# Residual add and RMS norm on one core: x and results moved in two interleaved partition groups in place of four, and the last residual on SyncE's queue

## The chip, the cores and the metric

One core of a Trainium2 chip. The metric is device time in microseconds (us), the median of several runs.

## The reference

x and residual are [32, 2048, 2048] float32, 537 MB each, and so is the output.

```python
z = x + residual
rms = np.sqrt(np.mean(z ** 2, axis=-1, keepdims=True) + eps)
return (z / rms * gamma).astype(np.float32)
```

## The kernel before

The 65,536 rows go through in 65 tiles. Tiles 1 to 63 have 128 partitions x 8 rows (8 MB each of x, residual and output); tile 0 has 3 rows a partition and tile 64 has 5. There are two buffers `z` for x, which also become the output in place, and one area for the residual. Three engines' programs carry it. SyncE moves x and the output:

```python
Q = 4
def group(q):
    return slice(q, P, Q)          # every fourth partition

def sp_turn(sp, i):
    def load(q):
        sp.wait_ge(s_out[q], i * U)      # store group q of tile i-1 has landed
        load_x(sp, i + 1, q)             # into the same partitions of the same buffer
    Turn(i).wait(sp, "done", -1)         # tile i-1 is computed
    for q in range(Q):
        store(sp, i - 1, q)
    for q in range(Q):
        load(q)
```

`sp_turn` is unrolled for i from 1 to 63. VectorE waits for x and residual of a tile, adds in three parts (`add_a`, `add_b`, `add_c`) and later scales. ScalarE squares and sums, and issues the residual of the next tile as soon as the adds have freed its place:

```python
def act_turn(s, t, chain):
    ...
    t.wait(s, "add_a")
    squares(s, chain, z[p], a, m, ssq[p][0], 0)
    if i == last - 1:
        load_r(s, t, 1)              # the last residual, on ScalarE's queue
    elif i:
        t.wait(s, "add_b")
        load_r(s, t, 1)
    ...
```

At the end SyncE stores tile 63 in two halves by rows, and tile 64 in three parts.

## Time and profile before

| | before |
|---|---|
| time | 3732.35 us (3732.1 to 3732.79, 4 runs) |
| bytes moved | 1610.73 MB, mean 432 GB/s |
| VectorE busy | 2300.7 us, 62% |
| ScalarE busy | 1059.7 us, 28% |
| data DMAs | 517 on SyncE's queue, 63 on ScalarE's |
| a tile's period | 58.00 to 58.02 us early, 58.16 us late |

Read it from the DMA rows: compute has room, DMA has none (its two data queues take 67.3% and 32.6% of the engines' time). The page's lines stand in the prediction. One that is not there is that of the queue which the profile names "instruction"; its columns are packets, MB and share of 16 engines' time:

```profile
q14 instruction: 7, 0.05, 0.0%
```

It looks like nothing. It matters below, because its packets take time from data: the one at 1426 us lasts 0.31 us, and the 64 KB packet that follows it on its engine 2.83 us in place of 2.42. (Six of the seven are of 8 KB and come during the run; one of 40 bytes comes at the start.) What the packets hold the trace does not show; that their number goes with the length of SyncE's program was my reading of their distance of 930 us.

### The profile page before, as it was taken

How to read it: one execution, taken by the hardware profiler on the slowest of the kernel's cores; microseconds unless marked ns; L12 is line 12 of the kernel's file. 1: busy time of each engine (PE TensorE's matmuls, PEld its weight loads, DVE VectorE, ACT ScalarE, POOL GpSimd, SP SyncE). 2: the span in 40 equal slices, each digit the busy share in tenths (PEclk: the TensorE clock that was granted, in tenths of full speed). 3: DMA queues.
4: the chain of work that ended last, by engine and by line, in shares of the span. 5: the costliest groups of instructions: out<-in, count | busy, mean ns of one | idle time of the engine just before them, and what ended most of it. 6: DMA issues, size and time to landing. Idle time of an engine off the chain costs nothing.

```text
span 3730.9 us, 4005 instructions
## 1 busy us (share of the span) xinstructions
DVE 2300.7 (62%) x842; ACT 1059.7 (28%) x1157; POOL 0.2 (0%) x4
## 2 busy tenths in 40 slices
DVE  5657566575665756657556575565755657556566
ACT  2323233232331322313223132231322313223132
POOL 0000000000000000000000000000000000000000
DMA  9999999999999999999999999999999999999998
GB/s 421 433 436 429 436 432 433 437 430 437 430 436 436 431 436 430 436 433 433 437 430 436 433 433 437 430 436 431 434 436 430 438 430 436 434 432 429 435 429 377
DMA packets 34695, 1610.73 MB, mean 432 GB/s; under 512 B 9281, under 2 KB 9345, under 8 KB 9345
## 3 DMA queue, kind: packets, MB, share of 16 engines
q1 hardware_dynamic: 25616, 1085.34, 67.3%
q10 hardware_dynamic: 9072, 525.34, 32.6%
q14 instruction: 7, 0.05, 0.0%
HBM read 1073.77 MB, written 536.87 MB: 432 GB/s over the span
## 4 chain that ended last, share of the span: by engine, by line
DMA 65%; DVE 27%; issue 5%; SPq 1%; ACT 1%; another core or an unknown queue 1%; ACTq 0%; DVEq 0%
DMA out_dram<-z 33%; DMA z<-in_x_dram 30%; DVE z L193 13%; DVE z L198 13%; SPq L170 1%; DMA r_area<-in_residual_dram 1%; ACT sq_junk L244 0%; DMA z<-in_gamma_dram 0%; ACTq L161 0%; DVE rstd L217 0%; ACT rms L254 0%; DVEq L314 0%; DVEq L139 0%; SPq L290 0%
## 5 line engine op out<-in xcount | busy, mean ns | idle before, releaser
L193 DVE TENSOR_TENSOR z<-z,r_area 128x8192 f32<-128x8192 f32 (+2 forms) x192 | 1104.8, 5810 | 1339.8 <-DMA z<-in_x_dram 1325.1
L244 ACT ACTIVATE sq_junk<-z 128x2048 f32<-128x2048 f32 x512 | 962.1, 1879 | 2640.9 <-DVE z L193 2630.7
L198 DVE SCALAR_TENSOR_TENSOR z<-z,rstd,gamma_tile 128x2048 f32<-128x2048 f32 x507 | 1156.5, 2344 | 4.5
L244 ACT ACTIVATION_READ_ACCUMULATOR sq_junk<-z 128x1 f32 x512 | 95.4, 186 | 0.0
L217 DVE RECIPROCAL rstd<-rms 128x4 f32<-128x4 f32 (+1 forms) x128 | 22.4, 175 | 58.2 <-ACT rms L254 58.2
L254 ACT ACTIVATE rms<-ssq,eps_tile 128x4 f32<-128x4 f32 (+1 forms) x128 | 38.0, 297 | 11.7
L198 DVE SCALAR_TENSOR_TENSOR z<-z,tail_rstd,gamma_tile 128x2048 f32<-128x2048 f32 x5 | 11.6, 2346 | 0.1
L311 DVE LOAD_MASK_SELECT gamma_tile<-z x1 | 0.0, 14 | 16.2 <-DMA z<-in_gamma_dram 16.2
L193 DVE TENSOR_TENSOR z<-z 128x2048 f32<-128x2048 f32 x3 | 6.7, 2284 | 0.0
L311 DVE STREAM_SHUFFLE gamma_tile<-z 128x2048 f32<-128x2048 f32 x1 | 2.3, 2290 | 0.0
L309 DVE MEMSET z<- 128x2048 f32 x1 | 1.8, 1765 | 0.4 <-issue 0.4
L244 ACT ACT_TABLE_LOAD x1 | 1.3, 1283 | 0.9 <-SPq L80 0.9
L254 ACT ACT_TABLE_LOAD x1 | 1.3, 1283 | 0.1
L254 ACT ACTIVATE tail_rms<-tail_ssq,eps_tile 128x2 f32<-128x2 f32 (+1 forms) x3 | 0.9, 295 | 0.1
L308 DVE MEMSET eps_tile<- 128x1 f32 x1 | 0.1, 59 | 1.0 <-SPq L80 1.0
L327 DVE RECIPROCAL tail_rstd<-tail_rms 128x2 f32<-128x2 f32 (+1 forms) x3 | 0.5, 158 | 0.0
L381 POOL MEMSET const-bfloat16-1.0<- 128x1 bf16 x1 | 0.1, 101 | 0.0
L381 POOL MEMSET const-uint8-127<- 128x1 uint8 x1 | 0.1, 101 | 0.0
L381 POOL MEMSET const-float32-0.0<- 128x1 f32 x1 | 0.1, 98 | 0.2 <-issue 0.2
L381 POOL MEMSET const-float32-1.0<- 128x1 f32 x1 | 0.1, 98 | 0.0
## 6 DMA issues: line engine op xcount, KB each, us to landing
out_dram<-z SPq DMA_DIRECT2D x2, 4096.0 KB, 27.5
z<-in_x_dram SPq DMA_DIRECT2D x4, 1280.0 KB
r_area<-in_residual_dram ACTq DMA_DIRECT2D x1, 5120.0 KB, 25.6
out_dram<-z SPq DMA_DIRECT2D x2, 2048.0 KB, 8.7
z<-in_x_dram SPq DMA_DIRECT2D x249
out_dram<-z SPq DMA_DIRECT2D x248, 30.6
z<-in_x_dram SPq DMA_DIRECT2D x1, 3072.0 KB
z<-in_residual_dram SPq DMA_DIRECT2D x1, 3072.0 KB, 17.2
```

Of the source, the lines that this page charges most:

```text
L170: sp.dma_start(out=rows(o_f, i)[group(q)], in_=z[i % 2][group(q), : sizes[i], :]).then_inc(s_out[q], U)
L193: return v.tensor_add(out=s, in0=s, in1=res(i, a, b))
L198: ins = v.scalar_tensor_tensor(out=s, in0=s, scalar=rs[:, c + g - a : c + g - a + 1], in1=gamma_tile[:, :], op0=mult, op1=mult,)
L217: v.reciprocal(out=rstd[p][h][:, :n], in_=rms[p][h][:, :n]).then_inc(dve, U)
L244: s.activation(out=sq_junk[:, :], in_=src[:, g, :], func=Act.Square, accum_out=sq[:, c + g - a : c + g - a + 1],)
L254: return s.activation(out=rm, in_=sq, func=Act.Sqrt, bias=eps_tile[:, :], scale=inv_d)
L308: v.memset(eps_tile[:, :], float(eps))
L309: v.memset(stage, 0.0).then_inc(tail_ev["add"], 1)
L311: v.stream_shuffle(gamma_tile[:, :].rearrange("p (a b) -> p a b", a=16), stage, [0] * 32)
L327: v.reciprocal(out=tail_rstd[:, a:b], in_=tail_rms[:, a:b]).then_inc(dve, U)
L381: nc = _bacc.Bacc("TRN2", target_bir_lowering=False, num_devices=1)
```

## The change

The intent is to move the same bytes with fewer DMAs. Two things change: the group count, and who issues the last tile's residual.

```diff
-    Q = 4
+    Q = 2
...
         for q in range(Q):
             store(sp, i - 1, q)
         for q in range(Q):
+            if i == last - 1 and q == Q // 2:
+                Turn(i).wait(sp, "add_a")
+                load_r(sp, Turn(i), 1)
             load(q)
...
-        if i == last - 1:
-            load_r(s, t, 1)
-        elif i:
+        if 0 < i < last - 1:
             t.wait(s, "add_b")
             load_r(s, t, 1)
```

## The prediction

> **What bounds the kernel now.** I read the page first: busy shares, the strip of 40 slices, the DMA queues.
>
> ```profile
> span 3730.9 us, 4005 instructions
> DVE 2300.7 (62%) x842; ACT 1059.7 (28%) x1157; POOL 0.2 (0%) x4
> DMA  9999999999999999999999999999999999999998
> GB/s 421 433 436 429 436 432 433 437 430 437 430 436 436 431 436 430 436 433 433 437 430 436 433 433 437 430 436 431 434 436 430 438 430 436 434 432 429 435 429 377
> DMA packets 34695, 1610.73 MB, mean 432 GB/s; under 512 B 9281, under 2 KB 9345, under 8 KB 9345
> q1 hardware_dynamic: 25616, 1085.34, 67.3%
> q10 hardware_dynamic: 9072, 525.34, 32.6%
> ```
>
> No compute engine is near full, the 16 DMA engines are in every slice but the last, and the rate is flat. x, residual and output are 536.9 MB each, so the bytes cannot shrink. The two queues' shares sum to 99.9% of the engines' time: this is a DMA-bound kernel with almost no holes.
>
> Next the waits, VectorE and ScalarE first, then SyncE's queue:
>
> ```profile
> ACT sq_junk L244 <- DVE z L193: 2630.7, 127, 41.1
> DVE z L193 <- DMA z<-in_x_dram: 1325.1, 63, 22.0
> ...
> SPq L149 <- DMA out_dram<-z: 2371.5, 252, 24.1
> SPq L170 <- DVE z L198: 1017.8, 63, 30.0
> ```
>
> VectorE waits for x in all 63 later tiles (21 us each), and SyncE waits 252 times (63 tiles x 4 groups) for a store group to land before it loads x into the place. These waits are long, but they cost nothing unless a DMA engine's ring runs dry behind them. So I looked at single packets in the trace. A whole 64 KB row goes as one packet. Following one engine's packets, the step from one packet's start to the next is 2.414 us, or 2.420 us when a completion write (the 4-byte packets) lies between. One tile of 8 rows is 24 such packets on each engine, with 9 completions: 24 x 2.414 + 9 x 0.006 = 57.99 us, and first landings of successive stores are in fact 58.00 us apart in most tiles. Up to the tail, no hole over 1 us was found on any engine. The steady state is at its floor.
>
> The end is different. Stretches near the end, columns VectorE, ScalarE and GpSimd busy, clock, DMA share, GB/s:
>
> ```profile
> 3700.00:3707.00 7.00, 7.00 (x3) 4.39 (x6) 0.00 (x0) 1.00 1.04 449
> 3707.00:3714.00 7.00, 6.93 (x6) 6.37 (x8) 0.00 (x0) 1.00 0.17 75
> 3714.00:3727.00 13.00, 6.91 (x4) 0.00 (x0) 0.00 (x0) 1.00 0.96 404
> 3727.00:3731.00 4.00, 0.00 (x0) 0.00 (x0) 0.00 (x0) 1.00 0.04 14
> ```
>
> The hole of 7 us is not shared by all. The 16 landings of a store group spread over 1.3 us at tile 1, 4.4 us at tile 20 and 10.8 us at the last group; the next slowest engine is then only 4.1 us behind the first. One engine is late. In the hole the other engines wait for the last tile's first output, while the late one still writes the second to last tile (17.51 us after 3700) and goes on without a pause to the end at 3729.7. The kernel is as long as this one engine's chain of packets. It fell behind in three ways: in the first ten tiles; in single jumps of about 0.74 us around 1426, 2360 and 3291 us, each at an 8 KB packet of the instruction queue; and, after the first of these jumps, by running at 58.16 us a tile in place of 58.01 (packets of 2.424 to 2.455 us), about 6 us over the last 40 tiles.
>
> [...] the page of the profile shows 9,281 packets under 512 B, and 580 data DMAs x 16 = 9,280. [...] both queues' packets last 2.418 us. [...] groups of every fourth take the same 2.418 us a packet as the whole-tile residual. So I expect full rate from groups of every second. That is the one thing that the trace of before does not show directly.
>
> **The change part by part.**
>
> *Two groups in place of four.* It removes two stores and two loads in each of 63 tiles: 252 DMAs, 252 completions on each engine x 6 ns = 1.5 us off every engine's chain. Data packets stay 64 KB rows. On the path: yes, the late engine is never idle.
>
> *Fewer SyncE instructions.* A tile is 8 of SyncE's DMA instructions before and 4 after. The instruction packets came every 930 us, 16 tiles, so SyncE's program uses up one per 16 tiles; halved, one per 32. About two fewer jumps of 0.74 us: 1.5 us.
>
> *Coarser credit.* SyncE issues the load of group 0 when store group 0 has landed on all engines. Behind it, the late engine still has one store group, 4 packets or 9.7 us, which covers SyncE's issue (0.5 to 0.6 us each) and the start of a transfer. So the late engine does not run dry. A fast engine may lead it by 3 groups x 2 packets x 2.42 = 14.5 us before, but only by 4 packets = 9.7 us [...] after, some 8 us. At a lead of 10.8 to 14 us the fast engines will have to stop in some late tiles. This lies beside the late engine's work and costs nothing at the end.
>
> *The last residual.* Before, ScalarE issued it at 3666.6 us and it interleaved with stores and x. After, it goes out on SyncE's queue behind the first x half, once the add of tile 63's first four rows is done (add starts near 3653.8 us, plus 8.7 = 3662.5 us, before the store group lands that SyncE waits for anyway). The late engine's list from 3653.8 on is the same set: stores 19.3, x 12.1, residual 12.1, stores 19.3, last stores 12.1 us. Only the order differs, and add of the last tile needs both x and residual. Worth 0 within 1 us.
>
> Sum: 1.5 + 1.5 + 0 = 3 us. I add 1 us for the chance that the late engine stays under the lag from which it ran at 58.16 us a tile (it began when the lag passed 4.9 us, two packets, which was the size of a group; with groups of four packets or later jumps it may begin later, or never, worth up to 6 us). 3732.2 - 4 = 3728 us.
>
> **The rivals.** [...] packets get longer than 2.418 us. For it: the untried shape. Against it: four groups show no trace of that. If it happened with a tenth of SyncE's queue packets, time would go up in proportion; at 5% longer packets on 2/3 of the bytes, 3.3%, 3855 us.
>
> *The wait takes over.* If halves make rings run dry [...], each tile pays a hole. For it: the lead that before tolerates is already larger than the 8 us left. Against it: the late engine paces the issue and always has 9.7 us queued. At 0.5 us a tile it would be 32 us: 3762 us.
>
> *The tail gains.* If the last x and residual land earlier, the hole of 7 us closes. For it: the change touches exactly that place. Against it: the late engine has no hole, so order cannot shorten its list. With the lag gone too, the best case is about 8 to 9 us: 3722 us.
>
> *Larger gain from fewer waits.* 2371 us of SyncE's waiting halves in count, but it was waiting beside a full DMA; nothing on the path.
>
> **Range and chances.** A floor of 1,536 row packets x 2.414 us = 3708 us, plus completions and the start and tail, leaves less than 0.6% to win, so faster by over 2% is out of reach: 0.004. Slower by over 2% (over 3807 us) [...]: 0.02. Range 3721 to 3735 us: the low end is the late engine cured, the high end 3 us of new holes.
>
> **What would show it.** Right: 252 x 16 = 4,032 packets fewer (30,663), row packets still 2.418 us, tile period 58.0 us with a mean of 432 or 433 GB/s, SyncE's store waits 126 in number at about the same sum, spread of landings capped near 8 us, two instruction packets fewer. The hole of 7 us before the last outputs stays, perhaps narrower. Wrong: row packets longer than 2.43 us in the SyncE queue, slices under 425 GB/s in the middle, the period over 58.2 us, or the last x landing more than 5 us away from 3698 us.

Full rate from groups of every second partition was expected from the measured 2.418 us of every fourth, and the 8 us is my estimate (the spread measured after is 6.5 us). In the trace before, SyncE begins to issue a load 0.02 us after the last landing that it waits for, and the last tile's first store has its first packet 0.83 us after its issue begins (3713.80 to 3714.63 us). A ring that "runs dry" means a DMA engine without a packet to move. Slower by over 2% was given 0.02, for longer packets or for a hole of more than 1.1 us in every tile. The sum: 1.5 + 1.5 + 0 = 3 us, with 1 us for the drift 4 us, and 3732.2 - 4 = 3728 us.

## The result

3728.09 us (3727.49 to 3728.51, 4 runs) against 3732.35 us. The ratio is 0.9988, with a 95% interval of 0.9971 to 1.0006. (A ratio is the mean time of one kernel's fast runs over that of the other's of the same rounds, so it is not quite the ratio of the medians.) The interval includes 1, yet the slowest run after is 3.6 us below the fastest before, and the experiments below repeat the difference. The predicted time was 3728.0.

The page of the changed kernel, first lines that answer to those of before:

```profile
span 3726.7 us, 3783 instructions
DVE 2300.5 (62%) x842; ACT 1059.8 (28%) x1157; POOL 0.2 (0%) x4
DMA  9999999999999999999999999999999999999999
GB/s 416 428 436 433 434 436 430 437 430 438 429 438 432 435 436 430 437 430 438 429 438 431 435 436 430 438 429 438 428 438 430 436 434 433 430 436 428 438 431 396
DMA packets 30660, 1610.70 MB, mean 432 GB/s; under 512 B 5248, under 2 KB 5312, under 8 KB 5312
q1 hardware_dynamic: 21728, 1090.57, 67.7%
q10 hardware_dynamic: 8928, 520.10, 32.3%
q14 instruction: 4, 0.03, 0.0%
```

The small packets have gone from 9281 to 5248 and the 8 KB packets of the instruction queue from 6 to 4 (the page's 7 counts one of 40 bytes); 5 MB (the last residual) went over from q10 to q1. Everything else is as it was. The last slice rose from 377 to 396 GB/s. The waits of VectorE and of SyncE's queue (us in total, times, longest us):

```profile
DVE z L197 <- DMA z<-in_x_dram: 1278.9, 61, 21.8
DVE z L197 <- DMA r_area<-in_residual_dram: 56.6, 3, 19.7
...
SPq L149 <- DMA out_dram<-z: 2407.7, 126, 30.0
SPq L170 <- DVE z L202: 1115.6, 63, 30.3
```

Half as many waits for store groups, at the same total: they ran beside a full DMA before and still do.

At the end of the run (columns as in the prediction's stretches):

```profile
3700.00:3707.00 7.00, 6.96 (x4) 6.87 (x11) 0.00 (x0) 1.00 0.93 403
3707.00:3710.50 3.50, 3.46 (x4) 2.28 (x4) 0.00 (x0) 1.00 0.22 94
3710.50:3723.00 12.50, 6.25 (x4) 0.00 (x0) 0.00 (x0) 1.00 0.97 410
3723.00:3726.70 3.70, 0.00 (x0) 0.00 (x0) 0.00 (x0) 1.00 0.03 13
```

The hole in which most DMA engines wait for the last tile's first output is half as wide, about 3.5 us in place of 7, and starts at about the same moment. The late engine again has none: its share of tile 63's second store lands at 3713.4 us and its last packet at 3725.6 us, 12.2 us later, which is the 12.1 us of data in the last tile's stores.

**Where the 4.2 us came from.** VectorE's add of a tile starts when the last engine has landed its x, so the times between successive starts are the clock of whichever engine is last. The adds of tiles 63 and 64 (start, length, what, idle time before and what ended it), before and after:

```profile
3653.80 17.36 DVE L193 TENSOR_TENSOR z<-z,r_area 128x8192 f32<-128x8192 f32 x3 [21.38 <-DMA z<-in_x_dram]
3698.09 10.96 DVE L193 TENSOR_TENSOR z<-z,r_area 128x4096 f32<-128x4096 f32 x3 [8.39 <-DMA z<-in_x_dram]
...
3650.53 17.36 DVE L197 TENSOR_TENSOR z<-z,r_area 128x8192 f32<-128x8192 f32 x3 [21.32 <-DMA z<-in_x_dram]
3693.93 10.96 DVE L197 TENSOR_TENSOR z<-z,r_area 128x4096 f32<-128x4096 f32 x3 [7.50 <-DMA z<-in_x_dram]
```

All starts, read from the trace of each kernel:

| | before | after | difference |
|---|---|---|---|
| start of tile 24's add | 1383.7 us | 1384.3 us | +0.6 |
| tiles 24 to 63, above 58.00 us a tile: single jumps | 2.08 us (0.61, 0.73, 0.74) | 0.57 us (0.39, 0.18) | -1.5 |
| the same: the rest, a steady drift | 6.0 us (58.16 us a tile) | 3.6 us (58.11 us a tile, from tile 29 on) | -2.4 |
| from tile 63's add to tile 64's | 44.29 us | 43.40 us | -0.9 |
| from tile 64's add to the end | 32.79 us | 32.80 us | 0 |
| sum | | | -4.2 |

The jumps of before come at 1426, 2360 and 3291 us, where the trace has 8 KB packets of the instruction queue; the one of 0.39 us after comes at 2850 us, beside such a packet too (0.18 us comes six tiles later without one). Between 200 and 3600 us there are four such packets before and two after. In tile 62 the spread of a store group's 16 landings is 10.8 us before in the first three groups and 14.3 us in the fourth; after, it is 6.5 and 6.3 us.

The landings of single engines show more than the clock. The engine that ends last does not begin to drift at tile 24 or 29: it falls back from the early tiles on, while another engine, late from the start, is still the last and hides it. Before, it is 2.45 us behind the first engine at tile 12 and 4.12 us at tile 23, 0.15 us a tile; after, 0.89 us at tile 10, 1.55 us at tile 16, 2.20 us at tile 17 and 3.42 us at tile 28, 0.11 us a tile but for the step at tile 17. That step is the instruction packet at 992 us, which the clock does not show. So the instruction packets run on this same engine. At 1426 us in the kernel before, the packet takes 0.31 us of it, and the 64 KB packet behind it lasts 2.83 us in place of 2.42: 0.72 us together.

### The profile page after: what moved, and what is told of

The parts are those of the page before. It is cut to its first block, busy times and chain, and to the rows that moved or that the text cites. A ratio compares the mean times of both kernels' runs of the same rounds, so it can differ in the third digit from the quotient of the medians.

```text
span 3726.7 us, 3783 instructions
## 1 busy us (share of the span) xinstructions
DVE 2300.5 (62%) x842; ACT 1059.8 (28%) x1157; POOL 0.2 (0%) x4
## 2 busy tenths in 40 slices
DMA packets 30660, 1610.70 MB, mean 432 GB/s; under 512 B 5248, under 2 KB 5312, under 8 KB 5312
## 4 chain that ended last, share of the span: by engine, by line
DMA 66%; DVE 27%; issue 4%; ACT 1%; another core or an unknown queue 1%; SPq 0%; ACTq 0%; DVEq 0%
DMA out_dram<-z 32%; DMA z<-in_x_dram 31%; DVE z L197 14%; DVE z L202 12%; DMA r_area<-in_residual_dram 3%; ACT sq_junk L248 0%; SPq L170 0%; DMA z<-in_gamma_dram 0%; ACTq L161 0%; DVE rstd L221 0%; ACT rms L258 0%; DVEq L315 0%; DVEq L139 0%; SPq L291 0%
```

## The experiments

Two theories stood at the start. A: the changed kernel shortens the late engine's chain all along the run, by fewer instruction packets, a slower drift and fewer completions. B: it gains at the end, by the order of the last residual. Others were added on the way, and the expectations name them.

Twelve kernels, all with the right result. Each was timed beside the kernel before on the same chip (medians 3732.39 to 3732.59 us), except two.

### One part at a time

Two groups alone, with the residual left on ScalarE:

```diff
 kernel before
-    Q = 4
+    Q = 2
```

> Two groups alone; the last residual stays on ScalarE's queue. Theory A (the late DMA engine's chain is shortened all along: fewer instruction packets, slower drift, fewer completions): most of the gain is here, 3728.3 to 3729.5 us against 3732.3, with at most 1 us missing. Rival B (the gain comes from the order of the last residual): close to the kernel before, 3731 us or more.

Measured: 3728.27 us (3727.58 to 3728.68, 5 runs), ratio 0.9988. The whole gain is here. Its clock looks like that of the changed kernel: 58.11 us a tile late, one jump at 2850 us, 43.35 us from tile 63's add to tile 64's.

The residual's part alone:

```diff
 changed kernel
-    Q = 2
+    Q = 4
```

> Four groups as before, the last residual on SyncE's queue between the second and the third x group. Theory A: nothing to gain by order, 3731.3 to 3732.6 us, six instruction packets in the run as before. Rival B: 3729.5 us or less.

Measured: 3732.89 us (3732.58 to 3734.5, 5 runs), ratio 1.0002, 0.3 us above theory A's range. Rival B falls. SyncE's queue and ScalarE's near the end, first the kernel before, with the residual at 3666.60:

```profile
3658.60 18.46 SPq L149 DMA_DIRECT2D z<-in_x_dram  x4
3680.48 9.58 SPq L175 DMA_DIRECT2D out_dram<-z  x2
...
3666.60 0.33 ACTq L161 DMA_DIRECT2D r_area<-in_residual_dram  x1
```

then this run, all of it on SyncE's queue (columns: start, length, what; several issues are merged):

```profile
3658.61 5.35 SPq L149 DMA_DIRECT2D z<-in_x_dram  x2
3664.01 0.60 SPq L161 DMA_DIRECT2D r_area<-in_residual_dram  x1
3668.33 5.36 SPq L149 DMA_DIRECT2D z<-in_x_dram  x2
3680.51 9.59 SPq L175 DMA_DIRECT2D out_dram<-z  x2
```

The residual is issued 2.6 us earlier, the last x group 3.4 us earlier (it starts at about 3673.2 in place of 3676.6), and it buys nothing: the late engine has the same list of packets to work off either way, and tile 63's stores follow at the same 3680.5.

### Is it the slack? One group, and two groups that wait for both

```diff
 changed kernel
-    Q = 2
+    Q = 1
```

> One group: a tile is stored whole and then loaded whole. SyncE's queue holds nothing while it waits for the store, but the residual on ScalarE's queue is still under way then (about 15 us of it). Theory A: fewer instruction packets still (2 or 3) and 3 completions per tile and engine in place of 5, so 3725.5 to 3728 us, no hole in the middle of the run. Rival C (each halving of the groups takes away slack, rings run dry): a hole of 2 us or more in every tile, tile period 60 us or more, 3850 us or more.

Measured: 3819.32 us (3809.39 to 3822.44, 5 runs), ratio 1.0231. A miss, and the instructive one. A tile takes 58.1 to 60.7 us after the start. In the tile from 1000 to 1059 us, two packets are stretched on most or all engines: the first residual packet after the store, near 1017 us (on eleven engines, 2.63 to 3.42 us in place of 2.42), and the last x packet, near 1054 us (on all 16, 2.58 to 3.57 us). One engine stands still for 0.76 us at 1017.5. My reason for expecting no hole was that the residual would be under way when the store ends. In fact ScalarE issues it at 1015.67 us and the store's data ends at 1017.0 to 1017.5 on the first engines: it is only just there. Whether emptiness or the whole-tile transfer is at fault, the next two runs tell.

```diff
 changed kernel, two groups
         def load(q):
-            sp.wait_ge(s_out[q], i * U)
+            for w in range(Q):
+                sp.wait_ge(s_out[w], i * U)
             load_x(sp, i + 1, q)
```

> The changed kernel's two groups and DMA shapes, but both x loads wait for both store groups, as the one load of one group did. Theory D (one group lost its 1.3 us a tile because SyncE's queue is empty when the store ends, so that nothing is there while the landing is told and the next load is issued): close to one group, 3795 to 3825 us, the packets at the ends of the store and of the load stretched. Rival E (one group lost it by the shape of its transfers: whole-tile DMAs of 128 partitions, lock step of the engines): close to the changed kernel, 3727 to 3731 us.

Measured: 3838.15 us (3833.23 to 3843.99, 4 runs), ratio 1.0288, above the range of theory D by 13 us and far from that of E. SyncE now waits once a tile:

```profile
SPq L182 <- DMA out_dram<-z: 2604.8, 63, 44.7
```

The page of this run:

```profile
DMA packets 30661, 1610.71 MB, mean 420 GB/s; under 512 B 5248, under 2 KB 5312, under 8 KB 5312
```

The DMAs, their shapes and their number are those of the changed kernel; only the wait moved, and 110 us went, 1.7 us in each of 63 tiles. In the trace, six engines stand still for 0.36 to 1.40 us at the end of a tile's store (near 1024.6 us), while SyncE issues the loads at 1026.75 us, about 2 us after the first engine has run out; the next residual, issued at 1022.90 us, has not begun on those engines either. So rival E falls, and that the two separate waits protect two groups is shown: with them, the second store group is still queued while the first one's landing is told and its load is issued. How the joined wait costs 1.7 us is shown only in part. Summed over all packets from 600 to 3500 us and averaged over the engines, a tile has 0.26 us of standing still and 0.54 us of longer residual packets at the end of the store, which fit theory D, and 0.83 us of longer x packets at the end of the load, which it does not explain. (In the changed kernel the three are 0.00, 0.03 and 0.03 us.)

```diff
 two groups that wait for both, x by one DMA
-            load_x(sp, i + 1, q)
+            if q == Q - 1:
+                whole_x(sp, i + 1)
```

> As the run before it, but x is loaded by one whole-tile DMA after both half stores. Theory D: again 3795 to 3825 us, the last load packet of a tile stretched. Rival E: if shape were all, this one is slow and the run before it is not.

Measured, once: 3836.17 us, 59.7 us in a typical tile. It is above the range by 11 us, and inside the range of the run before it (3833.23 to 3843.99): no sign that the shape of the load matters here. Why the last load packets of a tile are stretched as well, where a store is long queued behind them, these runs do not settle.

### More groups, and blocks of neighbours

```diff
 kernel before
-    Q = 4
+    Q = 8
```

> The kernel before with eight groups (the last residual on ScalarE's queue). 17 completions per engine and tile in place of 9, an instruction packet about every 8 tiles in place of 16, slack of 7 packets. Theory A: the four terms go the other way, 3 to 4 more jumps of 0.75 us and a steeper drift of the late engine (0.105 us a tile with two groups, 0.155 with four, so about 0.2 to 0.26 with eight): 3735 to 3742 us. Rival: if slack is what the late engine lacks, eight groups are no slower than four: 3732 us or less.

Measured: 6394.82 us (6365.44 to 6404.7, 4 runs), ratio 1.7114. A gross miss, and not for a term of theory A:

```profile
DMA packets 42762, 1610.80 MB, mean 252 GB/s; under 512 B 17344, under 2 KB 17408, under 8 KB 17408
q1 hardware_dynamic: 33680, 1085.37, 69.6%
```

The engines are busy all the time (the DMA strip is full) and move 252 GB/s. Their 64 KB packets on SyncE's queue have a median of 4.83 us in place of 2.42. Why groups of every eighth partition take twice as long, no run shows. I had cleared two groups by an argument from the partition pattern, and had not put it to eight.

```diff
 changed kernel
     def group(q):
-        return slice(q, P, Q)
+        return slice(q * (P // Q), (q + 1) * (P // Q))
```

> The changed kernel with each group a block of 64 neighbouring partitions in place of every second one. [...] SyncE's packets last up to twice 2.42 us: 4300 to 5500 us. [...] 3728 us within 2. [...]

(The two times are alternatives: packets lengthened by the blocks, or not. "Up to twice 2.42 us" was my estimate; the packets measured below take 5.05 us.)

Measured, once: 7326.07 us:

```profile
DMA packets 30660, 1610.70 MB, mean 220 GB/s; under 512 B 5248, under 2 KB 5312, under 8 KB 5312
q1 hardware_dynamic: 21728, 1090.57, 65.0%
q10 hardware_dynamic: 8928, 520.10, 34.2%
```

It is slower than my range because I stretched only SyncE's packets: the median is 5.05 us on SyncE's queue and also 5.05 us on ScalarE's, whose residual is still moved as a whole tile. So the rival of longer packets is real for other partition patterns, and groups of every second partition escape it: in the changed kernel the median packet is 2.418 us on both queues. What makes a pattern slow, these runs do not show.

### The instruction packets

The changed kernel, with its SyncE program padded by waits that are long met:

```diff
 changed kernel
         for q in range(Q):
             store(sp, i - 1, q)
+            if i > 1:
+                sp.wait_ge(s_out[1], (i - 1) * U)
+                sp.wait_ge(g_in, 4 * U)
+                sp.wait_ge(tail_ev["add"], 1)
```

> The changed kernel with three waits that are long met behind each store, so that SyncE's program is as long as before or longer, with the DMAs of the changed kernel. Theory A with instruction packets as one term: six or more instruction packets in the run, jumps of 0.5 to 0.9 us at some of them, 3728.8 to 3731 us. If the instruction packets do not matter (completions and drift carry all): 3728.1 us as the changed kernel, within 0.4 us.

Measured: 3729.65 us (3728.57 to 3730.69, 5 runs), 1.4 us more than two groups alone in the same rounds (3728.27); the two ranges just overlap, so the clock must decide. Between 200 and 3600 us there are three 8 KB instruction packets in place of two, at 595, 1661 and 2708 us (I had expected more), and the clock shows 58.83 us for the tile at 1661 and 58.83 and 58.61 us for two tiles at 2708. The drift is unchanged, 58.11 us a tile.

The other way, SyncE's turns 2 to 61 as a loop, which makes its program shorter (the definition of `sp_turn_looped` is left out here):

```diff
 kernel before
-        for i in range(1, last):
-            sp_turn(sp, i)
+        sp_turn(sp, 1)
+        with sp.Fori(0, last - 4, 2) as it:
+            for i in (2, 3):
+                sp_turn_looped(sp, i, it)     # the same DMAs and waits, rows and counts by `it`
+        for i in range(last - 2, last):
+            sp_turn(sp, i)
```

> The kernel before (four groups, residual on ScalarE's queue) with SyncE's turns 2 to 61 written as a loop of two[...]; the DMAs and waits are the same. Theory A (each instruction packet costs the late engine 0.6 to 0.9 us): the jumps near 1426, 2360, 3291 and 3659 us go, the drift of 0.155 us a tile stays: 3729 to 3730.5 us. If instruction packets cost nothing and what differs between two and four groups is the number of DMAs alone: 3732.4 us, within 0.5.

Measured: 3731.47 us (3730.53 to 3731.9, 5 runs), ratio 0.9997. The packets near 500, 1426, 2360 and 3291 us are gone, and no tile jumps at 2360 and 3291; one packet is left at 3564 us, and the tile there takes 58.87 us. But only 1 us was won of the 2 to 3 expected: tile 24's add starts 1.4 us later than in the kernel before, since the engine that is last there lost more in the early tiles. The late drift is 58.17 us a tile.

> The changed kernel with the same loop. Theory A: only the one jump of 0.4 us near 2850 us and a little beside it are left to win, drift 0.105 us a tile stays: 3726.8 to 3728 us, the best of all so far.

The edit is the same on the changed kernel. Measured: 3727.51 us (3726.84 to 3728.82, 5 runs), ratio 0.9987. No instruction packet between 200 and 3600 us, and no tile above 58.14 us after tile 7. It is the lowest median of all, but its range overlaps that of the changed kernel, so it isn't shown to be faster.

### The drift: stores or loads

Groups split apart: S store groups and Q load groups, each load waiting for the store groups that hold its partitions. Where there are four, they are issued in the order 0, 2, 1, 3 (left out below), so that the first two make up the first half.

```diff
 changed kernel
     Q = 2
+    S = 4                  # the other run: Q = 4, S = 2
-    def group(q):
-        return slice(q, P, Q)
+    def group(q, n):
+        return slice(q, P, n)
...
-            sp.wait_ge(s_out[q], i * U)
+            for w in range(S):
+                if w % min(Q, S) == q % min(Q, S):
+                    sp.wait_ge(s_out[w], i * U)
             load_x(sp, i + 1, q)
```

> The changed kernel with four store groups and two load groups (each load waits for its two store groups). Tells where the late engine's drift comes from. If it follows the number of stores: about 0.155 us a tile, 3730.5 to 3732 us (its SyncE program is also longer, so jumps as before). If it follows the number of loads or the slack: 0.105 us a tile, 3728 to 3730 us.

Measured, four store and two load groups: 3734.05 us (3733.21 to 3735.23, 4 runs), ratio 1.0005: slower than expected, and no better than before.

> The other way round: two store groups, four load groups. If the drift follows the stores: 0.105 us a tile, 3728 to 3730 us; if it follows the loads: 0.155, 3730 to 3732 us; if it follows all completions: 0.13 in this run and in the one before.

Measured, two store and four load groups: 3729.2 us (3728.66 to 3730.45, 4 runs), ratio 0.9992.

The clocks of all kernels with a full rate, from their traces (period of the last 20 full tiles, median):

| store / load groups | kernel | late period, us | instruction packets, 200 to 3600 us | add 63 to add 64, us |
|---|---|---|---|---|
| 4 / 4 | before | 58.16 | 4 | 44.29 |
| 4 / 4 | residual on SyncE | 58.16 | 4 | 44.17 |
| 4 / 4 | looped | 58.17 | 1 | 44.39 |
| 4 / 2 | | 58.16 | 4 | 43.61 |
| 2 / 4 | | 58.12 | 3 | 43.59 |
| 2 / 2 | changed | 58.11 | 2 | 43.40 |
| 2 / 2 | residual on ScalarE | 58.11 | 2 | 43.35 |
| 2 / 2 | padded | 58.11 | 3 | 43.39 |
| 2 / 2 | looped | 58.12 | 0 | 43.39 |

The drift follows the number of store groups in nine kernels, whatever the loads, the residual's queue and the program's length. It does not follow the slack: with four store and two load groups the spread of landings ends at 6.6 us, as in the changed kernel, and the drift is still that of four. Slack decides how far the others may run ahead, not how fast the late engine goes. The landings show the same climb of one engine from the early tiles in all nine, and all sixteen instruction packets between 1400 and 3600 us fell on that one engine. They are not its drift, which is 58.17 and 58.12 us a tile in the looped kernels, without them. What a store group costs the late engine, and why it is the engine of the instruction packets that pays, stays open; its stretched packets in the kernel before are stores, in the part of the tile where the other engines have gone on to loads (for example five of 2.43 to 2.46 us between 2605 and 2623 us).

## Why the prediction was right

The time was met to 0.1 us, and the picture held: one late engine that is never idle sets the end, and what shortens its chain shortens the kernel. Step by step, though, the terms were less exact than the sum. Two readings of the trace before were off. The spread of 10.8 us is that of the last tile's first three store groups; at the last group it is 14.3 us. And what fell behind in the first ten tiles was another engine than the one that sets the end.

- *Fewer completions, 1.5 us*: over-sized. The 4,035 packets fewer are there (34,695 to 30,660), but in tiles 12 to 24, where neither drift nor jumps show in the clock, the changed kernel gains 0.08 us on the one before, 0.007 us a tile and not 0.024. That is about 0.4 us in 63 tiles.
- *Fewer instruction packets, about two, 1.5 us*: right. Two fewer in the middle of the run, 1.5 us less in jumps; the padded and looped runs move the jumps with the packets.
- *The drift, 1 us as a chance*: under-sized and for a wrong reason. I tied its onset to a lag of 4.9 us, "two packets, which was the size of a group". There is no onset: the engine drifts from the early tiles and shows in the clock once it has passed the one that was last, at tile 24 before and at tile 29, with a lag of only 3.4 us, in the changed kernel. It is the slope that changed, 0.16 to 0.11 us a tile above 58.00, with the number of store groups, and it gave 2.4 us.
- *Coarser credit, no cost*: right. The spread stops growing at 6.5 us from tile 55 on, where I had said some 8: by this reading my estimate for issue and start was too small, since 9.7 - 6.5 leaves 3.2 us. That the separate waits protect it is shown by joining them: 110 us.
- *The last residual, 0 within 1 us*: right, by both runs that separate it. The last step from tile 63's to tile 64's add still became 0.9 us shorter; the table shows that this goes with the groups and not with the residual's queue. What in it does so isn't settled.
- *The start*: not in the sum. The changed kernel is 0.6 us later at tile 24. Its counterpart with the residual on ScalarE is 0.2 us later, so this is near what two kernels differ by there.

The forecast was -1.5 - 1.5 - 1 + 0 = -4; measured were +0.6 (start) - 1.5 (jumps) - 2.4 (drift) - 0.9 (last step) = -4.2, the small gain by completions lying within the start and the drift. That the sum hit within 0.1 us is luck: errors that cancel. Of the rivals, the longer packets and the wait that takes over were refuted for this change, and both are real a step further: eight groups cost 71% by packets of 4.83 us, one group 2.3% by the wait. The size that I gave the latter, 0.5 us a tile, was too small; it is 1.4 to 1.7 us a tile in the runs with one group and with joined waits.

## What to carry to other kernels

When DMA bounds a kernel and most of its engines idle at the end, look at the landings of single engines: here the slowest one's chain of packets was the time (its last packet landed at 3725.6 us of 3726.7, with no hole, while most others stood still for 3.5 us), and all that was won lay on that chain. In this kernel, halving the number of DMAs paid only as long as one more DMA was queued behind each wait for a landing. Time every partition pattern: a 64 KB packet took 2.418 us with every second or fourth partition, 4.83 us with every eighth, and 5.05 us in blocks of 64 neighbours. The step from four groups to two was worth 4 us, and the steps to one and to eight lost 87 and 2660 us.
